# The first of eight gate tiles formed by seven block products in place of two plain projections

## The chip, the cores and the metric

The kernel runs on one core of a Trainium2 chip. The metric is the device time of one execution in microseconds; the median of three runs is compared. All times below are read from one profiled execution of the kernel before, on its own clock, which starts at 0 with the span.

## The reference, cut to what matters

One encoder layer on 512 tokens of width 1024, in float32. The part around the change is the merge of two branches:

```
proj  = rms_norm(x) @ w_in                      # gates are its last 2048 columns
g_a, g_b = split(sigmoid(gates + b_gate))       # two gates of 1024 columns
merged = g_a * (y_a @ w_branch_a) + g_b * (y_b @ w_branch_b)
mix_out = merged @ w_out
```

`y_a` (512 columns) is the gated MLP branch, `u * (W_s LN(v) + b_s)`, and `y_b` (512 columns) the attention branch. Before the merge stand the projections of v, q and k, the attention, and the gMLP's v and u; behind it w_out, two norms, and an MLP of width 4096.

## The kernel before

Every large product is made in three float32r matmuls: each operand is split into a high part (a copy on ACT, `hi`) and a low part (a subtraction on DVE, `lo`), and hi·hi, hi·lo and lo·hi are added in PSUM. So every weight tile costs an ACT copy and a DVE subtraction before PE (TensorE) can use it. PE computes with activations transposed: a tile of 128 output columns stands on the partitions, the 512 tokens lie along the free side.

**The gate stage.** The 1024 merged columns are made in eight tiles d = 0..7 of 128 columns. A tile needs two projections of the normed input (gate a and gate b, depth 1024 each) and two branch products (depth 512 each, `branches`, lines 773 to 782). Two ways of making the two projections stand in the code:

- Plain (lines 784 to 790, only for d < `GSTD`, which is 1): the two weight tiles are split whole (`wsplit`, ACT 128x1024 and DVE 128x1024 each), and PE runs 2 x 8 x 3 = 48 matmuls of 128x512.
- Seven products (`seven_pairs`, lines 347 to 374, for the seven tiles from `GSTD` on): depth and tokens are halved, the two gates form the third pair of halves, and a Strassen-like scheme gets the four output blocks from seven products of quarter size. Each `product` (lines 341 to 345) is 4 x 3 = 12 matmuls of 128x256. Products 1, 2 and 4 take plain quarters of the weights (tiles `ar0`, `a12`, `ar1`); 6, 5, 3 and 7 take sums of quarters, which `seven` (lines 328 to 339) forms on DVE in a tile `s` (lines 331, 332, 336) and splits in two pieces: the first, called s12 here, serves products 6 and 5, the second, s34, products 3 and 7. Partial sums stand in three PSUM banks X, Y, Z; ACT snapshots `p1` and `z5`, and DVE joins them.

**What sets the order.** The program is written once, in the order of the code; a scheduler then deals the instructions to the five engines when the kernel is built, going by its own estimate of when each could run, with the order of the code as priority. On the chip each engine takes its instructions strictly in the order it was given, and waits where one must wait. So a matmul whose operand is late holds up all matmuls behind it.

**Buffers.** `wpool` has three slots of 8 KB a partition for the tag `raw`, in which the raw weights of a gate tile (`gw`) and its sums `s` take turns. The high and the low parts of the sums have three slots each (`whi`, `wlo`). `ar0`, `ar1`, `a12`, and the split branch weights `b0`, `b1` have one slot each in `gapool`, which is opened where the attention's memory is given back. Of the eight PSUM banks four (tag `acc`) hold X-, Y- and Z-like sums in turn: for the gMLP's u tiles (`pf`, `pg`) before, and for Y and Z of the gate tiles after. A bank is free once DVE or ACT has read it out.

**DMA.** SP (SyncE) issues in its order: the raw gate weights `gw` of tiles 0, 1 and 2 (two transfers of 512 KB each), then `bw` of tile 0 (the raw branch weights, two transfers of 256 KB), and so on. A `gw` is issued when a slot of `wpool` is given back, and what is queued behind it on SP waits with it.

**Ahead of the gate stage** stand four u tiles (lines 691 to 715): 24 matmuls each into `pf`, a GELU shared by ACT and DVE (`gelu2`, lines 651 to 656, tiles `gt` and `u`), a spatial product `pg` (line 710), two DVE steps into `sv` (lines 712 and 714), and a split of `sv` into `yah`, `yal` (line 715, recorded at lines 79 and 80). The last u tile's GELU and split fall into the time of gate tile 0.

## Time and profile before

| | |
|---|---|
| median of three runs | 779.86 us (779.51 to 780.35) |
| profiled execution, its own time | 781.44 us |
| its span (first to last instruction) | 779.6 us |
| PE busy | 769.1 us, 99% of the span |
| DVE, ACT busy | 602.1 us, 460.3 us |
| gate tile 0, plain: its 48 matmuls | 287.53 to 298.51 us |
| gate stage, from there to the first matmul of w_out | 287.53 to 412.80 us |

The page gives each engine's busy time and the share of the span. A timeline lists instructions in order of time: start, duration, engine, line of the code, operation, what is written and read, and in square brackets how long the engine sat idle just before and what it waited for. Consecutive matmuls overlap in the records, so the pace of PE is the distance of starts, not the duration. A table by stretches gives the busy time of each engine in each. A line number such as L345 is that of the kernel before; in the kernel after, lines behind the change stand five higher (L717 there is L712 here).

### The profile page before, as it was taken

To read this page: it belongs to the slowest core of one execution; us is meant where nothing else is said; L and a number is where in the kernel's file an instruction comes from. 1 tells how busy PE (TensorE), PEld (TensorE's weight loads), DVE (VectorE), ACT (ScalarE), POOL (GpSimd) and SP (SyncE) were. 2 spreads that over 40 slices of the span, in tenths; PEclk is the share of its full clock that TensorE was granted. 3 is DMA by queue.
4 is the path that set the end of the run, shared out by engine and by line. 5 is a ranking of instruction groups with operands and counts; after the bars stand their busy time and mean duration, and the time that the engine had idled before them with its cause. 6 is when DMAs were issued, how large, how long until landed. Compare 5 with 4: busy or idle time off the path is not lost.

```text
span 779.6 us, 12286 instructions
## 1 busy us (share of the span) xinstructions
PE 769.1 (99%) x4821; PEld 692.1 (89%) x4821; DVE 602.1 (77%) x963; ACT 460.3 (59%) x747; POOL 90.2 (12%) x124
## 2 busy tenths in 40 slices
PE   8999999999999999999999999999999999999996
PEld 5888999999988888999998899999999988888885
DVE  5785589888664887868756469998888699978784
ACT  5442558978776546545544457566666766655670
POOL 2301200010103500000000210011211100203010
PEclk9999999999999999999999999999999999999998
DMA  9643744253725533433544614469998998979703
GB/s 316 229 121 108 217 108 109 55 141 103 205 93 129 155 82 82 109 82 101 147 158 135 216 62 155 140 205 279 213 266 215 246 302 310 198 248 215 216 0 109
DMA packets 104749, 128.30 MB, mean 165 GB/s; under 512 B 3265, under 2 KB 75233, under 8 KB 103794
## 3 DMA queue, kind: packets, MB, share of 16 engines
q1 hardware_dynamic: 83920, 83.50, 34.3%
q0 software_dynamic: 20480, 43.61, 23.0%
q8 instruction: 38, 0.62, 0.3%
q10 hardware_dynamic: 290, 0.40, 0.1%
q14 instruction: 21, 0.17, 0.1%
HBM read 117.53 MB, written 26.74 MB: 185 GB/s over the span
## 4 chain that ended last, share of the span: by engine, by line
PE 98%; DMA 1%; issue 0%; DVE 0%; POOL 0%; ACT 0%; POOLq 0%; DVEq 0%; ACTq 0%
PE pacc L995 13%; PE pg L345 10%; PE pd L1086 6%; PE pd L1087 6%; PE pd L1088 6%; PE pgacc L345 6%; PE pf L85 5%; PE pf L84 5%; PE pf L86 5%; PE ptp L995 5%; PE pv L84 4%; PE pv L85 4%; PE pv L86 4%; PE pgS L345 3%; PE pd L84 2%; PE pd L86 2%
## 5 line engine op out<-in xcount | busy, mean ns | idle before, releaser
L1087 PE MATMUL pd<-hl,hhl 128*128 128x512 f32 x224 | 87.2, 389 | 0.0
L1088 PE MATMUL pd<-hl,hhl 128*128 128x512 f32 x224 | 87.0, 389 | 0.0
L1086 PE MATMUL pd<-hl,hhl 128*128 128x512 f32 x224 | 84.7, 389 | 0.0
L995 PE MATMUL pacc<-nt,hl 128*128 128x256 f32 x504 | 66.1, 279 | 0.0
L995 PEld LDWEIGHTS pacc<-nt,hl 128*128 128x128 f32 x504 | 62.0, 188 | 0.1
L1088 PEld LDWEIGHTS pd<-hl,hhl 128*128 128x128 f32 x224 | 42.0, 188 | 8.8
L1086 PEld LDWEIGHTS pd<-hl,hhl 128*128 128x128 f32 x224 | 42.0, 188 | 8.7
L1087 PEld LDWEIGHTS pd<-hl,hhl 128*128 128x128 f32 x224 | 42.0, 188 | 8.6
L74 ACT ACTIVATE hi<-s 128x1024 fp32r<-128x1024 f32 x30 | 31.7, 1059 | 29.3 <-DVE s L332 8.4
L80 DVE TENSOR_TENSOR hl<-dnw,hl 128x1024 fp32r<-128x1024 f32 x32 | 38.4, 1220 | 8.8 <-ACT hl L79 8.8
L75 DVE TENSOR_TENSOR lo<-s,hi 128x1024 fp32r<-128x1024 f32 x30 | 36.6, 1223 | 10.7 <-ACT hi L74 10.6
L79 ACT ACTIVATE hl<-s 128x1024 fp32r<-128x1024 f32 x28 | 29.4, 1057 | 25.8 <-DVE s L978 18.8
L84 PE MATMUL pf<-nh,hi 128*128 128x512 f32 x112 | 44.3, 396 | 0.0
L79 ACT ACTIVATE hl<-dnw 128x1024 fp32r<-128x1024 f32 x32 | 33.0, 1053 | 18.8 <-DMA dnw<-in_w_down_dram 10.9
L995 PE MATMUL pacc<-n,hl 128*128 128x256 f32 x336 | 44.1, 279 | 0.0
L86 PE MATMUL pf<-nh,lo 128*128 128x512 f32 x112 | 44.1, 393 | 0.0
L85 PE MATMUL pf<-nl,hi 128*128 128x512 f32 x112 | 44.0, 393 | 0.0
L995 PEld LDWEIGHTS pacc<-n,hl 128*128 128x128 f32 x336 | 41.4, 188 | 0.0
L80 DVE TENSOR_TENSOR hl<-s,hl 128x1024 fp32r<-128x1024 f32 x28 | 34.2, 1220 | 5.2 <-ACT hl L79 5.2
L1076 DVE TENSOR_TENSOR hhl<-hid,hhl 128x1024 fp32r<-128x1024 f32 x24 | 29.3, 1221 | 10.7 <-ACT hhl L1075 10.6
L85 PE MATMUL pv<-lo,nh 128*128 128x512 f32 x96 | 37.6, 391 | 0.0
L86 PE MATMUL pv<-hi,nl 128*128 128x512 f32 x96 | 37.3, 391 | 0.0
(382 smaller groups left out, 2257.4 us busy)
## 6 DMA issues: line engine op xcount, KB each, us to landing
upw<-in_w_up_dram SPq DMA_DIRECT2D x16, 1024.0 KB, 5.6
qkw<-in_w_in_dram SPq DMA_DIRECT2D x24, 512.0 KB, 5.3
dnw<-in_w_down_dram SPq DMA_DIRECT2D x12, 1024.0 KB, 7.2
gw<-in_w_in_dram SPq DMA_DIRECT2D x16, 512.0 KB, 5.5
t3d<-in_w_down_dram POOLq DMA_DIRECT2D x8, 1024.0 KB, 8.6
t1d<-in_w_down_dram POOLq DMA_DIRECT2D x8, 1024.0 KB, 9.8
slab<-in_w_in_dram SPq DMA_DIRECT2D x6, 1024.0 KB, 10.9
tsum<-in_w_down_dram POOLq DMA_DIRECT2D x6, 1024.0 KB, 9.8
```

Of the source, the lines that this page charges most:

```text
L74: nc.scalar.activation(hi, raw, AF.Copy)
L75: (sub or nc.vector).tensor_tensor(lo, raw, hi.bitcast(F32), op=ALU.subtract)
L79: nc.scalar.activation(hi, src, AF.Copy)
L80: return sub.tensor_tensor(lo, src, hi.bitcast(F32), op=ALU.subtract)
L84: nc.tensor.matmul(ps, ah, bh, start=start, stop=False)
L85: nc.tensor.matmul(ps, ah, bl, start=False, stop=False)
L86: return nc.tensor.matmul(ps, al, bh, start=False, stop=stop)
L345: nc.tensor.matmul(ps, a[:, j], b[:, j], start=first and not (j or i), stop=(j == KH - 1 and i == 2), skip_group_check=True)
L995: ins = nc.tensor.matmul(ps, a[:, j], b[:, j], start=first and not (j or m), stop=(j == KH - 1 and m == 2), skip_group_check=True)
L1086: nc.tensor.matmul(ps, ah, bh, start=start, stop=False, skip_group_check=True)
L1087: nc.tensor.matmul(ps, ah, bl, start=False, stop=False, skip_group_check=True)
L1088: return nc.tensor.matmul(ps, al, bh, start=False, stop=stop, skip_group_check=True)
```

## The change

`GSTD` goes from 1 to 0, so that tile 0 is made by the seven products too. In `seven_pairs` the first tile (the one without a `tail`) is written in another order: product 1, then 2 (the two products of plain weights that open and close bank X), and then product 6; for the other tiles the order of the code is as it was.

```diff
@@ seven_pairs
             Y, Z, X = banks()
-            product(6, Y, w, moving, True)
+            p1, z5, u2, u3 = snap("p1", two), snap("z5", 1), snap("u2", 1), snap("u3", 1)
             if tail:
+                product(6, Y, w, moving, True)
                 tail()
             product(1, X, w, moving, True)
-            p1, z5, u2, u3 = snap("p1", two), snap("z5", 1), snap("u2", 1), snap("u3", 1)
             nc.scalar.activation(p1, X, AF.Copy)
+            if not tail:
+                product(2, X, w, moving, False)
+                evac(i, c1[:, A], X)
+                product(6, Y, w, moving, True)
             nc.vector.tensor_tensor(u2, Y, p1, op=ALU.add)
             product(5, Z, w, moving, True)
             nc.scalar.activation(z5, Z, AF.Copy)
-            product(2, X, w, moving, False)
-            evac(i, c1[:, A], X)
+            if tail:
+                product(2, X, w, moving, False)
+                evac(i, c1[:, A], X)
             product(7, Y, w, moving, False)
@@ gate stage
-    GSTD = 1
+    GSTD = 0
```

What the scheduler makes of it shows at three places.

The first is PE, between the last matmuls of the last u tile and the first product of plain weights. Before, behind tile 0's two plain projections, tile 1's products 6 (`pgacc_3332`, bank Y) and 5 (`pgacc_3333`, bank Z) are followed by its product 1 (`pgS_3334`, bank X, weights `ar0_3318`):

```order
L345 MATMUL pgacc_3332<-nt_89,lo_3315 128x256
L345 MATMUL pgacc_3333<-nt_90,hi_3314 128x256 x2
L345 MATMUL pgS_3334<-nh_79,ar0_3318 128x256
L345 MATMUL pgS_3334<-nl_80,ar0_3318 128x256
L345 MATMUL pgacc_3333<-nt_90,lo_3315 128x256
L345 MATMUL pgacc_3333<-nt_90,hi_3314 128x256 x2
```

After, PE runs product 6 and 5 of tile 0 (`pgacc_3228`, `pgacc_3229`), then product 6 and 5 of tile 1 (`pgacc_3342`, `pgacc_3343`), and only then product 1 of tile 0 (`pgS_3230`, weights `ar0_3214`):

```order
L345 MATMUL pgacc_3343<-nt_90,hi_3324 128x256 x2
L345 MATMUL pgacc_3343<-nt_90,lo_3325 128x256
L345 MATMUL pgS_3230<-nh_79,ar0_3214 128x256
L345 MATMUL pgS_3230<-nl_80,ar0_3214 128x256
L345 MATMUL pgS_3230<-nh_79,ar0_3214 128x256 x2
```

So product 1 of tile 0, first in the code, is fifth on PE; behind it come tile 0's product 3, two matmuls of the branch product with `b0`, and product 2. The 48 matmuls of 128x512 are gone.

The second is DVE over the last u tiles. The numbers tell tiles apart: `yal_2747<-sv_3135` is the third u tile's split, `_3180` and `u_3169` belong to the fourth; before, `s_3311` are the sums of tile 1:

```order
L654 SCALAR_TENSOR_TENSOR gt_3125<-gt_3125,pf_3099 128x512
L656 SCALAR_TENSOR_TENSOR u_3124<-gt_3125,pf_3099 128x512
L714 SCALAR_TENSOR_TENSOR sv_3135<-sv_3135,u_3124 128x512
L80 TENSOR_TENSOR yal_2747<-sv_3135,yah_2746 128x512
L712 SCALAR_TENSOR_TENSOR sv_3180<-pg_3175,cols_65,sbias_2751 128x512
L75 TENSOR_TENSOR lo_3315<-s_3311,hi_3314 128x1024
L654 SCALAR_TENSOR_TENSOR gt_3170<-gt_3170,pf_3144 128x512
L656 SCALAR_TENSOR_TENSOR u_3169<-gt_3170,pf_3144 128x512
L714 SCALAR_TENSOR_TENSOR sv_3180<-sv_3180,u_3169 128x512
L75 TENSOR_TENSOR lo_3329<-s_3311,hi_3328 128x1024
L80 TENSOR_TENSOR yal_2747<-sv_3180,yah_2746 128x512
```

After, in the same stretch, from the sums of tile 1 (`s_3321`) to the low part of tile 0's `ar0`:

```order
L332 TENSOR_TENSOR s_3321<-s_3321,gw_3315 128x4x128
L719 SCALAR_TENSOR_TENSOR sv_3135<-sv_3135,u_3124 128x512
L336 TENSOR_TENSOR s_3321<-s_3321,gw_3315 128x4x128
L75 TENSOR_TENSOR lo_3325<-s_3321,hi_3324 128x1024
L659 SCALAR_TENSOR_TENSOR gt_3170<-gt_3170,pf_3144 128x512
L80 TENSOR_TENSOR yal_2747<-sv_3135,yah_2746 128x512
L717 SCALAR_TENSOR_TENSOR sv_3180<-pg_3175,cols_65,sbias_2751 128x512
L661 SCALAR_TENSOR_TENSOR u_3169<-gt_3170,pf_3144 128x512
L75 TENSOR_TENSOR lo_3339<-s_3321,hi_3338 128x1024
L719 SCALAR_TENSOR_TENSOR sv_3180<-sv_3180,u_3169 128x512
L80 TENSOR_TENSOR yal_2747<-sv_3180,yah_2746 128x512
L80 TENSOR_TENSOR ar0_3214<-gw_3201,ar0_3214 128x512
```

Tile 1's three sums (L331, one row ahead of this piece, L332, L336) have moved in among the GELU steps (before, they stood ahead of all this, where tile 0's sums now stand), and `sv_3180<-pg_3175`, which reads out the last u tile's PSUM bank, now stands behind the split of tile 1's s12. On ACT the copies for `ar0`, `ar1` and `a12` of tile 0 stand right behind the last u tile's `yah`, where those of tile 1 stood.

The third is SP. Before, with `gw_3201`, `gw_3305`, `gw_3419` and `gw_3585` the raw weights of tiles 0 to 3:

```order
L66 DMA gw_3305<-in_w_in_dram 128x8x128 x2
L66 DMA gw_3419<-in_w_in_dram 128x8x128 x2
L751 DMA bw_3204<-in_w_branch_a_dram 128x4x128
L751 DMA bw_3204<-in_w_branch_b_dram 128x4x128
L66 DMA gw_3585<-in_w_in_dram 128x8x128 x2
```

After, with `gw_3315` and `gw_3481` those of tiles 1 and 2, and `bw_3204` and `bw_3318` the branch weights of tiles 0 and 1:

```order
L66 DMA gw_3315<-in_w_in_dram 128x8x128 x2
L66 DMA gw_3481<-in_w_in_dram 128x8x128 x2
L756 DMA bw_3204<-in_w_branch_a_dram 128x4x128
L756 DMA bw_3204<-in_w_branch_b_dram 128x4x128
L756 DMA bw_3318<-in_w_branch_a_dram 128x4x128
```

The head of the queue is the same, but the slot that tile 2's `gw` takes is another. Before, it was the slot of tile 0's raw weights, given back by the second whole split of tile 0. After, tile 0's raw weights stay until `ar0`, `ar1` and `a12` are split; the sums of tile 0 and of tile 1 take turns in one slot, and tile 2's `gw` takes that slot once `lo_3339`, the last reader of tile 1's sums, is done. Tile 0's `bw` is still queued behind it.

## Prediction

> **What bounds the kernel now.** I read the page's busy times first, then what PE waited for (from 6 us on), then the table by stretches around the change.

> ```profile
> PE 769.1 (99%) x4821; PEld 692.1 (89%) x4821; DVE 602.1 (77%) x963; ACT 460.3 (59%) x747; POOL 90.2 (12%) x124
> ```
> ```profile
> PE pt L186 <- DMA ident<-in_ident_c_dram: 2.3, 1, 2.3
> PE pd L84 <- DVE gs L372: 0.5, 1, 0.5
> ```
> ```profile
> 285.00:290.00 5.00, 5.00 (x28) 4.29 (x27) 3.91 (x6) 2.18 (x3) 0.00 (x0) 1.00 1.14 299
> 290.00:295.00 5.00, 5.00 (x24) 4.14 (x23) 2.54 (x4) 2.58 (x4) 0.00 (x0) 1.00 0.05 10
> 295.00:300.00 5.00, 5.00 (x30) 4.38 (x29) 4.97 (x8) 4.99 (x8) 0.00 (x0) 1.00 0.00 0
> ```

> PE is the bound: behind its start it waits once in the whole span, 0.5 us at the end of the gate stage. In the stretch of the change PE (first number behind the length) is busy all the time, DVE (third) has about 4 us of slack in 290 to 300, and behind it is full. So a microsecond of matmul taken away here is a microsecond won, and a microsecond for which PE waits here is lost: no later idle of PE takes it up.

> **What is removed and added on PE.** Starts on the PE timeline, first of tile 0 as it is, then of products:

> ```profile
> 287.53 0.48 PE L84 MATMUL pf<-nh,hi 128*128 128x512 f32 x1
> ...
> 298.51 0.40 PE L345 MATMUL pgacc<-nt,hi 128*128 128x256 f32 x2
> ...
> 405.12 0.40 PE L345 MATMUL pgacc<-nt,hi 128*128 128x256 f32 x2
> ...
> 406.54 0.28 PE L345 MATMUL pgacc<-nh,hi 128*128 128x256 f32 x1
> ...
> 407.98 0.40 PE L84 MATMUL pf<-yah,b 128*128 128x512 f32 x1
> ```

> The 48 matmuls of tile 0 take 298.51 - 287.53 = 10.98 us. Two products of 12 matmuls take 1.42 and 1.44 us; I take 1.42. Seven are 9.94 us (10.08 by the other). PE is given 1.04 us less work (0.90 at least).

> **Whether the operands are there.** I follow the new order from 282 us on, where the order on DVE begins to differ, on the clock of before, with durations from these rows of DVE, ACT and PE:

> ```profile
> 270.40 1.22 DVE L331 TENSOR_TENSOR s<-gw 128x1024 f32<-128x1024 f32 x1
> 283.26 0.68 DVE L654 SCALAR_TENSOR_TENSOR gt<-gt,pf 128x512 f32<-128x512 f32 x1
> 287.81 0.75 DVE L712 SCALAR_TENSOR_TENSOR sv<-pg,cols,sbias 128x512 f32<-128x512 f32 x1 [0.36 <-PE pg L710]
> 300.14 0.68 DVE L80 TENSOR_TENSOR b<-bw,b 128x512 fp32r<-128x512 f32 x1
> 300.75 1.22 DVE L75 TENSOR_TENSOR lo<-s,hi 128x1024 fp32r<-128x1024 f32 x1
> 301.88 0.68 DVE L80 TENSOR_TENSOR b<-bw,b 128x512 fp32r<-128x512 f32 x1
> ```
> ```profile
> 283.98 0.63 ACT L655 ACTIVATE gt<-gt 128x512 f32<-128x512 f32 x1 [2.04 <-DVE gt L654]
> 286.75 1.06 ACT L74 ACTIVATE hi<-s 128x1024 fp32r<-128x1024 f32 x1
> 296.52 1.14 ACT L79 ACTIVATE ar<-gw 128x512 fp32r<-128x512 f32 x2
> 297.56 0.62 ACT L79 ACTIVATE a<-gw 128x512 fp32r<-128x512 f32 x1
> ```

> On DVE a 512-wide step frees the engine after 0.60 us (300.14 to 300.75) and its result is there after 0.68; a 1024-wide one after 1.13 and 1.22. On ACT 0.52 and 0.62, and 1.06 for 1024. A hand-over between engines I take as 0.05 us.

> Wait A, a PSUM bank. PE ends products 6 and 5 of tile 0 at 287.53 + 2 x 1.42 = 290.37; their s12 has long been split. Product 6 of tile 1 then writes the bank that held the last u tile's `pg`, read out by L712. Before, that read ended at 288.56. Now DVE, from 283.26: gt to 283.86; tile 1's L331 to 284.99; u to 285.59; L332 to 286.19; sv to 286.79; L336 to 287.39; the low part of s12, whose high part starts on ACT at 286.75 as the like row does now (a slot of `whi` opens then) and ends at 287.81, from 287.86 to 288.99; gt to 289.59; yal, done at 290.28; only then L712, 290.31 to 291.06. PE goes on at 291.11: it waits 0.74.

> Wait B and C, `ar0` of tile 0. DVE goes on: u to 291.58; the low part of tile 1's s34, whose high part must wait for the slot of tile 0's s12, read by PE until 290.5, so ACT 290.5 to 291.6 and DVE 291.65, done at 292.87, engine free at 292.78; sv, done at 293.47. On ACT the last yah follows from 293.52, then `ar0` high from 294.04 to 294.66; on DVE the last yal from 294.20, then `ar0` low from 294.80 to 295.49. PE has done products 6 and 5 of tile 1 at 291.11 + 2.84 = 293.95 and finds the high part at 294.71 (0.76 waited); two matmuls, 0.24, take it to 294.95, and the third wants the low part, there at 295.54 (0.59 waited). Product 1 ends at 296.72, product 3 at 298.14.

> Wait D, the branch weights. Next on PE stand two matmuls with `b0`, whose raw `bw` is queued on SP behind tile 2's `gw`. SP and transfers:

> ```profile
> 283.37 0.99 SPq L66 DMA_DIRECT2D gw<-in_w_in_dram  x2
> ```
> ```profile
> 337.83 0.99 SPq L66 DMA_DIRECT2D gw<-in_w_in_dram  x2
> 339.03 0.92 SPq L751 DMA_DIRECT2D bw<-in_w_branch_a_dram  x1
> ```
> ```profile
> gw<-in_w_in_dram SPq DMA_DIRECT2D x2, 512.0 KB, 4.8
> bw<-in_w_branch_a_dram SPq DMA_DIRECT2D x1, 256.0 KB, 5.6
> ```
> ```profile
> 300.25 0.99 SPq L66 DMA_DIRECT2D gw<-in_w_in_dram  x2
> 302.59 0.37 SPq L751 DMA_DIRECT2D bw<-in_w_branch_a_dram  x1
> ```
> ```profile
> 308.00 0.63 ACT L79 ACTIVATE b<-bw 128x512 fp32r<-128x512 f32 x1 [3.06 <-DMA bw<-in_w_branch_a_dram]
> ```
> ```profile
> bw<-in_w_branch_a_dram SPq DMA_DIRECT2D x1, 256.0 KB, 3.1
> ```

> Before, `gw` of tile 2 left at 283.37. Now it leaves when tile 1's s34 is split, at 292.92. Where the pair was issued with nothing between (337.83, transfers of the stretch 330 to 345), `bw` a left 1.20 us behind `gw` and landed 5.6 us later, 6.8 behind `gw`; in the group from 300.25 it landed at 308.0, 7.75 behind. The last row is the shortest of all, 3.1 us, a `bw` issued at 312.04 with no `gw` ahead. I take 6.8, since here too both are issued back to back: 299.72. ACT makes `b0` high, 0.63, and PE goes on at 300.45: it waits 2.31 us. With 7.75 it would be 3.26; with 3.1 us from its own issue at 294.12 `b0` would be ready at 297.9, no wait.

> Behind that I find nothing late. The low part of `b0` is wanted after 16 more matmuls, at 302.6; DVE stands in its queue at the sums of tile 2 until that `gw` lands (0.5 + 4.8 to 5.6 behind 292.92, so 299.0 at the latest), and makes it by 301.1. The other steps that tile 0 gains (`u2`, `u3`, the joins, `p1`, `z5`) are those of every other tile, where PE hides them in 15 us a tile. The table load of the sigmoid moves on ACT to behind `b1`, while PE has branch products and product 7.

> **The sum.** Waits 0.74 + 0.76 + 0.59 + 2.31 = 4.40, less 1.04: +3.36 us. The profiled span of 779.6 becomes 783.0. That execution took 781.44 us by its own time, 1.6 over the median of the runs, 779.86; I add the 3.36 to the median: 783.2 us. Bounds of the terms: A to C hang on a chain of steps measured to 0.02 us each and can move by some 0.4; D lies between 0 and 3.26. A measurement of this kernel tells about 0.2% (1.6 us) from no change.

> **Rivals.**

> The branch weights come in time. Then A, B and C remain: 2.09 - 1.04 = +1.05 us, 780.9, which is within 0.2%. It speaks for it that a `bw` by itself lands in 3.1 us; against it that all groups with 1 MB ahead on the queue are later. The decision lies at a landing before 297.4, 4.5 us behind the issue of `gw`: sooner than that `gw` itself was there in the stretch 330 to 345. Chance 0.10.

> No wait is left, and the smaller work shows: 778.8, 1.04 faster, also within 0.2%. The mechanism would be DVE and ACT running ahead: if the GELU of the last u tile were out 2 us sooner, bank, `ar0` and the issue of `gw` would all come sooner by that. The slack that DVE had in 290 to 300 speaks for it; against it that in the new order the sums fill just this slack, and that DVE's chain above has little idle in it, 0.47 us at s12 and 0.8 at the last yah. Chance 0.04, with 0.02 beyond 0.2%.

> PE's clock falls in the waits. These rows are from the start of the kernel, behind 2.27 us of waiting, and from the one later wait:

> ```profile
> 10.46 0.80 PE L84 MATMUL pv<-w0hi,nh 128*128 128x512 f32 x1
> ...
> 12.76 0.63 PE L86 MATMUL pv<-w0hi,nl 128*128 128x512 f32 x1
> 13.18 0.63 PE L84 MATMUL pv<-w0hi,nh 128*128 128x512 f32 x1
> ...
> 14.42 0.39 PE L84 MATMUL pv<-w0hi,nh 128*128 128x512 f32 x1
> 14.65 0.40 PE L85 MATMUL pv<-w0lo,nh 128*128 128x512 f32 x1
> ```
> ```profile
> 412.80 0.50 PE L84 MATMUL pd<-hi,mh 128*128 128x512 f32 x1 [0.52 <-DVE gs L372]
> 413.14 0.40 PE L85 MATMUL pd<-lo,mh 128*128 128x512 f32 x1
> ```

> Early matmuls start 0.42 us apart, from 14.42 on 0.23; after a wait of 0.52 there is at most one long step, 0.34. If the 2.3 us of D (or all four waits, 4.4 of 13 us) put PE back into the slow pace for as long as its first matmuls ran in it, 10.46 to 14.42 us, some nine of them, it would cost 9 x 0.19 = 1.7 more: +5.1, 785.0. Against it: none of my waits is as long as the slow stretch itself. Chance 0.13. [...]

> More is late than I see, in tiles 1 to 3, whose raw weights all arrive against the same queue. The row at 308.00 shows ACT waiting 3.06 us for a `bw` without PE feeling it; if that cover is gone, up to such a wait comes on top: +5 to +6, 785.5. Chance 0.07.

> **How the numbers follow.** The forecast, all four waits with D between 1.6 and 3.3, has a chance of 0.66: 782.5 to 784.2, likeliest 783.2. To hold 8 in 10 the range takes in part of the cases on both sides, from 781.6 (D cut to a third) to 785.1 (the clock). Slower by over 0.2% (above 781.4): forecast, clock and late tiles, 0.86 less 0.01 for small D, 0.85. Same: `bw` in time, half of no wait, and that 0.01: 0.13. Faster by over 0.2%: 0.02.

> **What would show it.** In the profile after, PE should have idle in 290 to 301 for the first time: before the first `pgacc` of tile 1 (released by DVE sv), before `pgS` (by ACT `ar0`, then DVE `ar0`), and the longest before the first `pf<-yah,b` (by ACT `b`, itself behind DMA `bw`); behind 301 PE should be full again until the end of the gate stage, which should come at about 416. SP should issue tile 2's `gw` near 293. If PE shows no idle at `pf<-yah,b`, wait D is wrong; if the matmuls behind it start 0.2 us apart for 128x256, the clock fell; if the stage's end is later by more than the idle in 290 to 301, it is a later tile.

## The result, and the profile after

| | before | after |
|---|---|---|
| median (lowest to highest), 9 executions each | 779.7 us (779.13 to 780.35) | 784.1 us (782.31 to 786.92) |
| profiled execution, its own time | 781.44 us | 784.1 us |
| its span | 779.6 us | 782.3 us |

The ratio is 1.0056, with a 95% interval of 1.0046 to 1.0065: 4.4 us slower. The executions after are not one group: four lie at 782.3 to 783.1 with a mean granted clock of 0.998 or 0.999, three at 784.1 to 784.7 with 0.997, two at 786.2 and 786.9 with 0.995 and 0.996. The profiled one is of the middle group. (The executions of before lie at 0.997 to 0.999 with no such grouping, so 0.997 alone tells nothing; the times do. The mean also takes in a granted clock of 0.50 behind PE's last matmuls, from 775.52 us on in the trace of before and from 780.42 in this one, where it holds nothing up.)

What PE waited for, from 6 us on, in the kernel after (engine, line, releaser, then us in total, times, longest):

```profile
PE pf L84 <- ACT b L79: 1.8, 1, 1.8
PE pgacc L345 <- DVE sv L717: 0.7, 1, 0.7
PE pt L186 <- DVE xn L182: 0.5, 1, 0.5
PE pd L84 <- DVE gs L377: 0.5, 1, 0.5
PE pgS L345 <- ACT ar L79: 0.4, 1, 0.4
PE pgS L345 <- DVE ar L80: 0.3, 1, 0.3
```

Four waits are new, and they are the ones forecast, in their places: D (`pf`), A (`pgacc`), B and C (`pgS`). The row of `pt` belongs to the start of the kernel: the profiled execution of before waited 2.3 us there, this one 0.5. So the clocks of the two traces differ: tile 0 starts at 285.87 here and at 287.53 before, 1.66 apart, and 1.66 is taken off whatever is compared. The PE timeline:

```profile
285.87 0.48 PE L345 MATMUL pgacc<-nt,hi 128*128 128x256 f32 x2
...
288.64 0.28 PE L345 MATMUL pgacc<-nt,lo 128*128 128x256 f32 x1
289.61 0.47 PE L345 MATMUL pgacc<-nt,hi 128*128 128x256 f32 x2 [0.70 <-DVE sv L717]
...
292.38 0.28 PE L345 MATMUL pgacc<-nt,lo 128*128 128x256 f32 x1
293.03 0.38 PE L345 MATMUL pgS<-nh,ar 128*128 128x256 f32 x1 [0.38 <-ACT ar L79]
293.25 0.28 PE L345 MATMUL pgS<-nl,ar 128*128 128x256 f32 x1
293.85 0.50 PE L345 MATMUL pgS<-nh,ar 128*128 128x256 f32 x2 [0.31 <-DVE ar L80]
...
296.45 0.28 PE L345 MATMUL pgacc<-nh,lo 128*128 128x256 f32 x1
298.58 0.50 PE L84 MATMUL pf<-yah,b 128*128 128x512 f32 x1 [1.85 <-ACT b L79]
298.92 0.42 PE L85 MATMUL pf<-yal,b 128*128 128x512 f32 x1
299.15 0.40 PE L345 MATMUL pgS<-nh,a 128*128 128x256 f32 x1
299.35 0.41 PE L345 MATMUL pgS<-nl,a 128*128 128x256 f32 x1
...
302.12 0.60 PE L86 MATMUL pf<-yah,b 128*128 128x512 f32 x1
302.55 0.40 PE L84 MATMUL pf<-yah,b 128*128 128x512 f32 x1
```

The idle in brackets counts from the modelled end of a matmul. What a wait costs is the distance of starts less the usual step of 0.12: A 0.85, B 0.53, C 0.48, D 2.01, in all 3.87 us. The first step behind each wait is longer as well, by some 0.1 (0.22 for 0.12 at 293.03, 0.34 for 0.23 at 298.58), 0.4 for the four. Then comes what the sum didn't hold: from 299.15 on, matmuls of 128x256 start 0.21 us apart and not 0.12, until 302.5. From 298.58 to 302.55 there are 17 matmuls; at the usual steps (0.34 for the first behind a wait, 14 of 0.118 and two of 0.23) they take 2.45 us, here 3.97: 1.52 more. By stretches (behind the length: PE, PEld, DVE, ACT, POOL busy, then the granted clock, the share of DMA, GB/s):

```profile
290.00:295.00 5.00, 4.31 (x34) 3.91 (x33) 4.29 (x7) 2.46 (x5) 0.00 (x0) 1.00 0.54 151
295.00:300.00 5.00, 3.15 (x22) 2.86 (x21) 2.67 (x4) 1.94 (x4) 0.00 (x0) 0.91 0.66 163
300.00:305.00 5.00, 5.00 (x25) 4.55 (x25) 4.15 (x7) 3.73 (x5) 0.00 (x0) 0.74 0.36 107
305.00:310.00 5.00, 5.00 (x32) 4.44 (x31) 3.06 (x5) 2.60 (x4) 0.00 (x0) 1.00 0.09 19
```

PE is idle in the first two, and in the third it is busy throughout at a granted clock of 0.74 with 25 matmuls: a full bar that hides most of the 1.52 us. The sum is 3.87 + 0.4 + 1.52 - 1.04 = 4.75. On PE, from the start of tile 0 to the first matmul of w_out, it is 416.00 - 285.87 = 130.13 after and 412.80 - 287.53 = 125.27 before, 4.86 more; 0.1 stays open. To the end of the span it is 4.36 more (496.43 after, 492.07 before), since what follows the last matmul's start took 6.6 us in this execution and 7.1 in that of before.

### The profile page after: what moved, and what is told of

The parts are those of the page before. It is cut to its first block, busy times and chain, and to the rows that moved or that the text cites. A ratio compares the mean times of both kernels' runs of the same rounds, so it can differ in the third digit from the quotient of the medians.

```text
span 782.3 us, 12375 instructions
## 1 busy us (share of the span) xinstructions
PE 770.8 (99%) x4857; PEld 694.7 (89%) x4857; DVE 607.0 (78%) x974; ACT 462.9 (59%) x753; POOL 89.8 (11%) x124
## 4 chain that ended last, share of the span: by engine, by line
PE 96%; DMA 1%; DVE 1%; issue 0%; ACT 0%; POOL 0%; SPq 0%; POOLq 0%; DVEq 0%; ACTq 0%
PE pacc L1000 13%; PE pg L345 10%; PE pd L1092 6%; PE pd L1093 6%; PE pd L1091 6%; PE pgacc L345 6%; PE ptp L1000 5%; PE pf L84 5%; PE pf L85 5%; PE pf L86 5%; PE pv L84 4%; PE pv L85 4%; PE pv L86 4%; PE pgS L345 3%; PE pd L84 2%; PE pd L86 2%
## 5 line engine op out<-in xcount | busy, mean ns | idle before, releaser
L74 ACT ACTIVATE hi<-s 128x1024 fp32r<-128x1024 f32 x32 | 33.8, 1059 | 37.1 <-DVE s L332 14.9
L75 DVE TENSOR_TENSOR lo<-s,hi 128x1024 fp32r<-128x1024 f32 x32 | 39.0, 1221 | 8.2 <-ACT hi L74 7.9
L80 DVE TENSOR_TENSOR hl<-dnw,hl 128x1024 fp32r<-128x1024 f32 x32 | 38.4, 1221 | 8.3 <-ACT hl L79 8.3
L79 ACT ACTIVATE hl<-s 128x1024 fp32r<-128x1024 f32 x28 | 29.4, 1058 | 26.1 <-DVE s L983 18.8
L79 ACT ACTIVATE hl<-dnw 128x1024 fp32r<-128x1024 f32 x32 | 33.0, 1053 | 19.3 <-DMA dnw<-in_w_down_dram 9.8
L80 DVE TENSOR_TENSOR hl<-s,hl 128x1024 fp32r<-128x1024 f32 x28 | 34.2, 1220 | 5.2 <-ACT hl L79 5.2
L84 PE MATMUL pf<-nh,hi 128*128 128x512 f32 x96 | 38.0, 396 | 0.0
L86 PE MATMUL pf<-nh,lo 128*128 128x512 f32 x96 | 37.8, 394 | 0.0
L85 PE MATMUL pf<-nl,hi 128*128 128x512 f32 x96 | 37.8, 394 | 0.0
L85 PE MATMUL pv<-lo,nh 128*128 128x512 f32 x96 | 37.6, 391 | 0.0
L86 PE MATMUL pv<-hi,nl 128*128 128x512 f32 x96 | 37.2, 391 | 0.0
## 6 DMA issues: line engine op xcount, KB each, us to landing
qkw<-in_w_in_dram SPq DMA_DIRECT2D x24, 512.0 KB, 5.2
gw<-in_w_in_dram SPq DMA_DIRECT2D x16, 512.0 KB, 5.2
```

What stands on the lines that cost most here:

```text
L74: nc.scalar.activation(hi, raw, AF.Copy)
L75: (sub or nc.vector).tensor_tensor(lo, raw, hi.bitcast(F32), op=ALU.subtract)
L79: nc.scalar.activation(hi, src, AF.Copy)
L80: return sub.tensor_tensor(lo, src, hi.bitcast(F32), op=ALU.subtract)
L84: nc.tensor.matmul(ps, ah, bh, start=start, stop=False)
L85: nc.tensor.matmul(ps, ah, bl, start=False, stop=False)
```

## The experiments

My theory after this trace: all four waits stem from one thing, `ar0` becoming ready only behind the whole tail of the last u tile; D is then a second-order wait, for a transfer behind `gw` on SP; and the half pace comes from D. The rivals: DVE's load is the reason; the transfer is late by the engines' load and not by the queue; the half pace comes from the sum of the waits; seven products are no less work.

**The branch weights on another queue.** Tile 0's `bw` goes by GpSimd's queue, the rest is the kernel after.

```diff
@@ gate_raw
-            nc.sync.dma_start(rawb[d][:, br], ...)
+            (nc.sync if d else nc.gpsimd).dma_start(rawb[d][:, br], ...)
```

> The kernel after, with the two transfers of tile 0's raw branch weights issued by GpSimd's queue and not behind tile 2's gate weights on SyncE's. My theory: wait D (2.0 us between the starts of matmuls in the trace after) is a matter of the queue alone and goes, but for some 0.4 us in which the low part of b0 may now be late; the clock fell because D was the longest wait, so it stays up too. Waits A, B and C stay at 0.85 + 0.53 + 0.48 = 1.86. 779.7 - 1.04 + 1.86 + 0.0 to 0.4 gives 780.5 to 780.9, and all its executions lie close together. Rival: the clock falls by the sum of the waits within some 10 us, not by the longest one; then matmuls start 0.21 us apart behind the third wait in some executions, and the time is 782 with a spread of some 2 us. Second rival: the landing is late by the 16 engines' load, not by the queue; then D stays and the time with it, 784.

Measured: 781.25 us (780.33 to 782.75, 11 executions) against 779.87 (28), ratio 1.002 [1.0011, 1.0029], +1.4. PE's waits in this kernel:

```profile
...
PE pgacc L345 <- DVE sv L717: 0.7, 1, 0.7
PE pd L84 <- DVE gs L377: 0.5, 1, 0.5
PE pgS L345 <- ACT ar L79: 0.4, 1, 0.4
PE pgS L345 <- DVE ar L80: 0.3, 1, 0.3
...
PE pf L86 <- DVE b L80: 0.2, 1, 0.2
```

and ACT's copy that made PE wait in D:

```profile
294.27 0.62 ACT L79 ACTIVATE b<-bw 128x512 fp32r<-128x512 f32 x1
```

A, B and C stand unchanged; D is gone, since `b0` is made at 294.27 with no wait ahead of it, against 297.90 in the kernel after. What is left of it is 0.2 us of idle for the low part. The two transfers now leave at 268.27 and 269.20, 24 us sooner than in the kernel after, and land at 271.9 and 273.0, long before tile 2's `gw` leaves at 291.30. So D came from where `bw` stood, behind that `gw` in SP's order. Whether it would also be late on a queue of its own, sharing the DMA engines with that `gw`, this run doesn't tell, because the two no longer move at the same time. The granted clock is 1.00 in each stretch of five microseconds from 280 to 310, and no execution has a mean clock below 0.997: three waits of 1.86 us together didn't halve it. The time is 0.35 above the top of what I expected, within the interval. The executions don't lie close together as expected: they spread over 2.4 us, and the two longest, 782.2 and 782.75, have a mean clock of 0.999. What lengthens them is not shown.

**Room of its own for `ar0`.** In the kernel after, `ar0` lies in `gapool`, and its split stands behind the last u tile's. My reading is that its place in that pool lies over buffers of the last u tile; which buffers is not shown, and it isn't so for the whole pool: `bw` of tile 0 lies there too, and on the other queue its transfers left at 268.27. Here a pool for `ar0` is opened before those buffers are given back:

```diff
+    arpool = pool(gp, "arpool")
     gst.close()
     gapool = pool(gp, "gapool")
@@ gate_weights
-    ... split1(src, tag, gapool)
+    ... split1(src, tag, arpool if tag == "ar0" else gapool)
```

> The kernel after, with ar0 in a pool of its own, in room that is free before the last u tile ends. The order of the program changes by that alone: product 1 of tile 0 stands right behind the last u tile on PE, with products 6 and 5 of tile 0 and 1, 6 and 5 of tile 1 behind it, and the branch product some 2 us of matmuls later than in the kernel after. My theory: waits A, B and C all come from ar0's room being freed late, and go; D is met by more work and shrinks to about 1.3, since SyncE issues tile 2's gate weights where it did. 779.7 - 1.04 + 1.3 gives 780.0 and no fall of the clock. Rival: any wait over 1 us in this place halves the clock, 1.5 us more: 781.5. Second rival: DVE is the reason for the waits, and they come back at other matmuls: 782 or more.

Measured: 780.66 us (780.24 to 781.78, 11 executions), ratio 1.0013 [1.0005, 1.0022], +0.8. PE's waits at the gate stage:

```profile
PE pf L84 <- ACT b L79: 1.3, 1, 1.3
...
PE pd L84 <- DVE gs L377: 0.5, 1, 0.5
```

A, B and C are all gone by this one change of room, and D is cut to 1.3 us of idle. For B and C the operand is there sooner: PE first uses `ar0` at 280.00, in the kernel after at 293.03. For A it isn't so: DVE still reads the last u tile's bank late,

```profile
289.96 0.74 DVE L717 SCALAR_TENSOR_TENSOR sv<-pg,cols,sbias 128x512 f32<-128x512 f32 x1
```

but PE now has product 1 of tile 0 and of tile 1 to run, and comes to product 6 of tile 1, which waited for that bank in the kernel after, only at 292.14. So A was covered, not removed, and D, with a cause of its own, is only shorter: the theory of one cause holds for A to C. DVE has the same work as in the kernel after, so its load alone does not make the waits; its order and PE's both changed. The time is 0.7 above the 780.0 expected: 0.2 is the reference of these runs, 779.87 and not 779.7, and 0.3 is D, which costs 1.47 between starts and 0.1 in the step behind it; the rest stays open. No execution has a mean clock below 0.997, and the traced one keeps 1.00 behind the wait: none of 11 shows the half pace at 1.3 us.

**Room for three tiles.** `ar0`, `a12` and `p1` in that pool, `ar1` in `gapool`:

```diff
@@ gate_weights
+    ... split1(src, tag, gapool if tag == "ar1" else arpool)
@@ seven_pairs' snapshots
-    lambda nm, nb: gapool.tile(...)
+    lambda nm, nb: (arpool if nm == "p1" else gapool).tile(...)
```

> As the run before, but ar0, a12 and the snapshot p1 are in the room that is free early, and ar1 is not. Products 1 and 2 of tile 0 can then both run before the branch product, which comes behind some 3 us more of matmuls. My theory: no wait is left at the start of the gate stage, and what remains is the smaller work of PE, 84 matmuls of 128x256 in place of 48 of 128x512: 779.7 - 1.04 = 778.7, faster than both kernels. Rival: the smaller work does not show, because DVE and ACT, which have more to do in seven products than in two plain projections, hold PE up later in the stage: 779.7 or more, with PE idle behind 305 us. Second rival: D stays, since the raw branch weights are issued as late as before: 780.7.

Measured: 778.76 us (777.98 to 779.34, 11 executions), ratio 0.9984 [0.9975, 0.9992]: 1.1 us faster than the kernel before (0.6 to 2.0 by the interval) and 5.3 below the kernel after. The transfers on SP leave no sooner than in the kernel after (`gw` at 292.77, there at 291.22), and ACT makes `b0` and `b1` late too:

```profile
292.77 0.99 SPq L66 DMA_DIRECT2D gw<-in_w_in_dram  x2
293.93 1.04 SPq L757 DMA_DIRECT2D bw<-in_w_branch_a_dram  x1
```
```profile
299.72 1.37 ACT L79 ACTIVATE b<-bw 128x512 fp32r<-128x512 f32 x2 [2.11 <-DMA bw<-in_w_branch_a_dram]
```
```profile
300.21 0.28 PE L345 MATMUL pgS<-nh,ar 128*128 128x256 f32 x1
300.40 0.50 PE L84 MATMUL pf<-yah,b 128*128 128x512 f32 x1
```

But PE reaches the branch product at 300.40, behind products 1, 2, 6 and 5 of tile 0, the same of tile 1 without its 2, and more, and finds `b0` there, made by 300.34. D's transfer was never made sooner; it was covered. With no wait left, the smaller work shows about as forecast: 1.1 us by the medians, and by the traces 0.84, from the first `pg<-nt,hi` (79.14 here, 80.69 before) to the first matmul of w_out (410.42 and 412.80), where 1.04, and 0.90 at least, was forecast.

**GSTD = 0 alone.** The kernel before with that one line, the first tile's products in the order of the others:

```diff
-    GSTD = 1
+    GSTD = 0
```

> The kernel before with GSTD = 0 and nothing else: the first tile's products are written in the order of the other tiles (6, 1, 5, 2). If the scheduler goes by when operands are there and not by the order of the code, the reordering of the first tile in the change did nothing, and this is the kernel after in all but name: 784.1 against 779.7, with the same waits at the same places. Rival: the order of the code does put products 1 and 2 sooner, so that without it the waits are longer: 785 or more.

Measured: 783.34 us (783.06 to 785.02, 5 executions), ratio 1.0056 [1.0042, 1.007]. The same four waits stand in its trace, D a little longer:

```profile
PE pf L84 <- ACT b L79: 2.2, 1, 2.2
...
PE pgacc L345 <- DVE sv L712: 0.7, 1, 0.7
...
PE pgS L345 <- ACT ar L79: 0.4, 1, 0.4
PE pgS L345 <- DVE ar L80: 0.3, 1, 0.3
```

And with the line numbers set aside, its instructions stand on every engine in the order of the kernel after. The part of the change that names the products of plain weights first does nothing here; that the scheduler puts them behind what is ready, since their operand has room last, fits this and the run with room for `ar0`. Its profiled execution has a granted clock of 0.998 and no half pace, so it is the four waits without a fall of the clock: 783.34, which is +3.7, and +3.4 and +3.6 in the two others of its kind (783.06 and 783.21 against 779.63); the two with 0.996 and 0.997 are at 784.95 and 785.02.

**One wait by itself: 1.9, 2.8 and 3.7 us.** In the kernel before, PE waits once in its middle, 0.52 us for the last read of a bank. Repeating that read (it writes the same values again) makes this wait longer, with PE full on both sides and no other wait near:

```diff
@@ tail of seven_pairs, last tile
-                nc.vector.scalar_tensor_tensor(c2[:, A], Y, ...)
+                for _ in range(4 if i == n - 1 else 1):      # 6 and 8 in the others
+                    nc.vector.scalar_tensor_tensor(c2[:, A], Y, ...)
```

> The kernel before, with the last read of the last gate tile's bank Y repeated five times more, which is 5 x 0.46 us of DVE work in a row ahead of the one wait of PE in the middle of the kernel (0.5 us at 412.3). That wait becomes one of 2.8 us, with PE full on both sides. It tells whether one wait of this length is enough to bring the clock down. If it is, the matmuls behind it run at half pace for some 3 us, as in the kernel after: +2.3 and +1.5, 783.5. If it takes several waits close together, or one longer than this: +2.3, 782.0. [...]

> The kernel before, with the last read of the last gate tile's bank Y repeated three times more: the one wait of PE in the middle of the kernel becomes 0.5 + 3 x 0.46 = 1.9 us, about as long as wait D in the kernel after (2.0 between starts, 1.85 idle). The wait alone costs 1.4: 781.2. Theory one: the clock looks back over a stretch of some 3.3 us (so long the half pace lasted in both traces that show it) and is halved when most of that was idle, wherever the stretch happens to begin; 1.9 of 3.3 is just over half, so a few of the executions at most show it, and the median is 781.2 to 781.6. Theory two: any wait of about this length halves the clock each time, 782.7. Theory three: it is the sum of several waits that counted in the kernel after, and one of 1.9 alone does nothing, 781.2 in every execution.

> As the run before, with seven repeats: a wait of 0.5 + 7 x 0.46 = 3.7 us, 3.2 more than before: 783.1 by the wait alone. Theory one (a look back over some 3.3 us): the wait covers most of a stretch wherever it begins, so every execution shows the half pace, 1.5 us more, some of them two stretches of it: 784.6 to 785.5, and none near 783.1. Theory two (a matter of chance that doesn't grow with the wait): executions both at 783.1 and at 784.6, as with the wait of 2.8. [...]

Measured, with the mean granted clock of each execution (the kernel before at 779.87 beside the wait of 2.81, at 779.63 beside the other two):

| wait | median | expected by the wait alone | executions | ratio |
|---|---|---|---|---|
| 1.89 us | 781.64 | 781.2 | 781.37, 781.46, 781.64, 782.36 (0.998); 784.23 (0.996) | 1.0032 [1.002, 1.0045] |
| 2.81 us | 782.78 | 782.0 | 781.64, 782.26, 782.48 (0.998); 783.08, 783.34, 784.46 (0.996) | 1.0033 [1.0021, 1.0045] |
| 3.73 us | 784.33 | 783.1 | 783.7, 784.01, 784.33, 785.11, 786.04 (0.995 to 0.997) | 1.0063 [1.0051, 1.0076] |

PE behind the wait of 1.89 us, in the one execution of five whose mean clock (0.996) points to the half pace, which is the profiled one:

```profile
413.10 0.50 PE L84 MATMUL pd<-hi,mh 128*128 128x512 f32 x1 [1.89 <-DVE gs L373]
413.44 0.39 PE L85 MATMUL pd<-lo,mh 128*128 128x512 f32 x1
413.67 0.52 PE L86 MATMUL pd<-hi,ml 128*128 128x512 f32 x1
413.99 0.63 PE L84 MATMUL pd<-hi,mh 128*128 128x512 f32 x1
414.41 0.63 PE L85 MATMUL pd<-lo,mh 128*128 128x512 f32 x1
...
416.97 0.49 PE L85 MATMUL pd<-lo,mh 128*128 128x512 f32 x1
417.31 0.39 PE L86 MATMUL pd<-hi,ml 128*128 128x512 f32 x1
```

and the stretch of half pace behind the wait of 2.81 us:

```profile
414.30:417.50 3.20, 3.20 (x10) 2.42 (x9) 1.85 (x3) 1.22 (x2) 0.00 (x0) 0.50 0.00 0
```

In these two traces the first matmuls behind the wait still run at full pace, then seven or eight start 0.42 us apart, then the pace is full again; the record of the granted clock has 0.50 for 3.41 us (413.78 to 417.19 and 414.24 to 417.65). One wait was enough here, without a sum of several. Not every execution shows it: by the mean clock and the time, none of 11 executions shows the half pace at 1.3 us (the run with room for `ar0`), 1 of 5 at 1.9, 3 of 6 at 2.8, all 5 at 3.7. The kernels with D beside other waits show it in 5 of 9 (D 1.85 us idle) and 2 of 5 (2.2 us, `GSTD` = 0 alone). So in these runs the share grows with the wait, but the counts are small. Theory two of the wait of 1.9, that such a wait halves the clock each time, is out: it did in 1 of 5.

Theory one, a look back over a stretch of some 3.3 us, can be sharpened from the traces. In the kernel after the record has a granted clock of 1.00 from 12.42 on (matmuls of 128x512 start 0.43 us apart before it, 0.23 behind), 0.50 from 299.14, 1.00 from 302.56 and 0.50 from 780.42: the three changes lie 84, 85 and 225 times 3.413 us behind the first. In the kernel before it has 1.00 from 14.35 and 0.50 from 775.52, 223 times 3.413 later. So in these two traces the changes fit stretches of 3.413 us that follow one another without a gap, called beats here. My reading is that it counts how much of one such beat PE was busy. Two of them (behind the length: PE busy, granted clock, DMA share, GB/s), the kernel after and `GSTD` = 0 alone, each with the beat that follows:

```profile
295.73:299.14 3.41, 1.56 (x11) 1.00 0.72 182
299.14:302.56 3.42, 3.42 (x17) 0.50 0.01 2
```
```profile
297.55:300.96 3.41, 1.97 (x14) 1.00 0.13 30
300.96:304.37 3.41, 3.41 (x23) 1.00 0.39 115
```

| trace | beat | PE busy, of 3.41 us | granted clock in the next beat |
|---|---|---|---|
| wait of 3.73 | 410.24 to 413.66 | 0.07 | 0.50 |
| wait of 2.81 | 410.83 to 414.24 | 0.90 | 0.50 |
| room for `ar0`, end of the kernel | 771.06 to 774.48 | 1.32 | 0.50 |
| wait of 1.89 | 410.36 to 413.78 | 1.53 | 0.50 |
| kernel after | 295.73 to 299.14 | 1.56 | 0.50 |
| other queue, end of the kernel | 771.29 to 774.70 | 1.72 | 1.00 |
| `GSTD` = 0 alone | 297.55 to 300.96 | 1.97 | 1.00 |
| room for `ar0` | 300.02 to 303.44 | 2.70 | 1.00 |

In these rows the clock falls behind a beat in which PE was busy for 1.56 us or less, and stays up behind one with 1.72 or more; half of a beat, 1.71, lies between, but no row shows that the limit is there. The wait of 2.2 us that an edge cuts in two (`GSTD` = 0 alone) left it up, the one of 1.89 that lies within one beat brought it down. The edges lie differently against the work: the clock falls 0.68 us behind the end of the wait of 1.89, 0.90 behind that of 2.81 and 0.37 ahead of that of 3.73. That it is this which makes some executions of a kernel show the half pace and others not is my reading. The median at 3.7, 784.33, is a little below the 784.6 expected: in its trace the clock falls at 413.66 and PE goes on at 414.03, so a part of the slow stretch lay in the wait and cost nothing.

## Why the prediction was right, point by point

- **PE's work, -1.04.** Borne out by the run with no wait left, -1.1 [-2.0, -0.6] by the times, -0.84 by the traces.
- **Waits A, B, C.** With the 1.66 us between the traces, PE was to go on at 289.45, 293.05 and 293.88; it did at 289.61, 293.03 and 293.85. They cost 0.85, 0.53 and 0.48 where 0.74, 0.76 and 0.59 were forecast, 1.86 in all against 2.09. The 0.1 by which the first step behind each wait is longer was left out of the sum. DVE's slack in 290 to 300, read as about 4 us, is 2.5 by the rows shown (5.00 - 2.54 and 5.00 - 4.97); the sum doesn't use it. The chain of DVE's steps was right:

```profile
288.71 0.75 DVE L717 SCALAR_TENSOR_TENSOR sv<-pg,cols,sbias 128x512 f32<-128x512 f32 x1
...
293.10 1.29 DVE L80 TENSOR_TENSOR ar<-gw,ar 128x512 fp32r<-128x512 f32 x2
```

- **Wait D.** SP and ACT:

```profile
291.22 0.99 SPq L66 DMA_DIRECT2D gw<-in_w_in_dram  x2
292.43 0.83 SPq L756 DMA_DIRECT2D bw<-in_w_branch_a_dram  x1
```
```profile
297.90 0.63 ACT L79 ACTIVATE b<-bw 128x512 fp32r<-128x512 f32 x1 [3.61 <-DMA bw<-in_w_branch_a_dram]
```

`gw` was forecast to leave at 291.26 on this clock and left at 291.22, `bw` 1.21 behind it (1.20 forecast); by ACT's start it was there at about 297.85, 6.6 behind `gw` and not 6.8. D cost 2.01, not 2.31.

- **Nothing later.** Behind 302.56 the clock is full and PE waits only once more in the gate stage, the 0.5 us of before at its end, so no later tile came late. The end was forecast at about 416 on the clock of before, which is 414.5 on this one; it came at 416.00, 1.5 later, by the half pace and the longer first steps, less what the waits fell short:

```profile
416.00 0.50 PE L84 MATMUL pd<-hi,mh 128*128 128x512 f32 x1 [0.51 <-DVE gs L377]
```

- **The rival that came as well: PE's clock.** The executions that keep the clock lie at 782.3 to 783.1 here and 783.1 to 783.3 with GSTD = 0 alone, within 0.9 of the forecast of 783.2. The median, 784.1, lies in the group with one stretch of half pace, which was priced at 1.7 and cost 1.52. So it is luck that 784.1 also lies in the 782.5 to 784.2 given for the waits alone: they came 0.53 short, and the half pace made more than that good. What was wrong is the chance of 0.13, and the reason given against it, that none of the waits is as long as the slow stretch: D left PE idle for 1.85 us of one beat of 3.41, and that was enough. The two executions near 786.5 fit two such stretches by their clock; no trace of one was taken, so that is not shown. What the runs with one wait add: 1.89 us of waiting alone brought the clock down in one execution of five.

What stays open: whether the limit is just half of a beat. The traces put it between 1.56 us busy of 3.41 (the kernel after) and 1.72 (the run with the other queue), with PE's ends as the profile models them.

## What to carry to other kernels

Where one engine is full to 99%, giving it less work is worth only what its operands' readiness allows: look up when the buffer of the first new operand becomes free before counting the matmuls saved. Here moving three small tiles to memory that is free sooner turned 4.4 us lost into 1.1 won, while naming the products first in the code moved nothing. It did so partly by covering waits: the bank and the transfer were as late as before, but PE had other work. And price a wait of PE not with its length alone: the half pace behind it cost 1.52 us in the kernel after, and it came in none of 11 executions at a wait of 1.3 us, 1 of 5 at 1.9, 3 of 6 at 2.8 and 5 of 5 at 3.7.
